# Linear attention on one core: V loads on the Activation queue, ten output buffers, stores three groups behind compute

## The chip, the cores and the metric

The kernel runs on one core of a Trainium2 chip. The metric is the device time of one execution in microseconds; a kernel is run several times and the median is quoted. A profile of one execution comes with each kernel; its span is about 1.8 us shorter than the time of that same execution. Executions over 1.5% slower than the fastest of the same kernel are left out of the means. A ratio is the mean time of one kernel's fast runs over that of the other's fast runs in the same rounds, so it is not quite the ratio of the medians.

The engines go by their names in the profile: PE multiplies matrices (PEld is its loading of weights), DVE is the vector engine, ACT the Activation (scalar) engine, POOL the general one, and SP issues transfers. A transfer (DMA) is issued by SP or ACT into that engine's queue, also called its ring or row, and moved in packets by 16 DMA engines. In a page's DMA row the span is cut into 40 slices, and each digit is the busy share of a slice in tenths (9 is 90% or more).

## The reference

Three float32 inputs of 8 x 12 heads x 512 rows x 64 columns, one output of the same shape.

```python
Q_feat = np.maximum(0, Q) + 1
K_feat = np.maximum(0, K) + 1
KV = np.einsum('bhkd,bhkv->bhdv', K_feat, V)
K_sum = np.sum(K_feat, axis=2)
numerator = np.einsum('bhqd,bhdv->bhqv', Q_feat, KV)
denominator = np.einsum('bhqd,bhd->bhq', Q_feat, K_sum)
return (numerator / (denominator[:, :, :, None] + 1e-10)).astype(np.float32)
```

There is little arithmetic per byte: 37.75 MB are read and 12.58 MB written.

## The kernel before

Four heads form a group; there are 24 groups. A group moves K, V and Q in and one output out, each as one transfer of 524,288 bytes (128 partitions x 2 runs of 2048 bytes). In iteration `it` the program prepares the features of group `it`, makes the products K'V and the transposes of Q for group `it-1`, divides and writes the output tile of group `it-2`, issues the loads of group `it+6` and the store of group `it-5`.

```python
IN_BUFS = 6
OUT_BUFS = 7
LAG = 5
...
    def load(g):
        k_raw = in_pool.tile([P, M, C, D], FP32, name="k_raw")
        ...
        nc.sync.dma_start(out=k_raw, in_=k_dram[:, sl])
        nc.sync.dma_start(out=v_raw, in_=v_dram[:, sl])
        nc.sync.dma_start(out=q_raw, in_=q_dram[:, sl])

    def store(g):
        nc.sync.dma_start(out=o_dram[:, g * M : g * M + M], in_=outs.pop(g))

    def features(g):
        ...   # kf on DVE (line 86), v_aug on ACT (line 89), qf on DVE (line 90)

    def kv_and_transpose(g):
        ...   # 32 small matmuls into kva_ps (line 107), copied by ACT (line 115);
        ...   # 8 transposes of qf into qt_ps (line 119), copied by ACT (line 121)

    def output(g):
        o_sb = out_pool.tile([P, M, C, D], FP32, name="o_sb")
        ...   # 32 small matmuls into o_ps (line 132); per half: reciprocal
        ...   # (line 142) and multiplication into o_sb (line 143), both on DVE

        for g in range(IN_BUFS):
            load(g)
        for it in range(NG + 2):
            if it < NG:
                features(it)
            if 1 <= it < NG + 1:
                kv_and_transpose(it - 1)
            if it >= 2:
                output(it - 2)
            if it + IN_BUFS < NG:
                load(it + IN_BUFS)
            s = it - 2 - (LAG - 2)
            if s >= 0:
                store(s)
        for s in range(NG + 2 - LAG, NG):
            store(s)
```

## Time and profile before

| what | value |
|---|---|
| time, median of 3 runs | 136.72 us (136.59 to 136.78) |
| busy: PE, DVE, ACT, SP's transfers | 44%, 51%, 40%, 99% of the span |
| transfers | 96 of 524,288 bytes, all on one queue |
| steady rate | 383 to 406 GB/s from 10 to 122 us |
| division waiting for a store to land | 38.5 us in 13 places |

Read it in this order: the DMA row shows that transfers bound the kernel, so idle time on an engine matters only where it delays a transfer. The prediction below shows the lines. One thing that it uses is in no summary line. A transfer runs on 16 DMA engines, and each reports its share with a count; the trace has the time of each count. The **last count** of a transfer is its landing. The **spread**, last count less first, is how far the slowest DMA engine is behind the fastest. I read a large spread at the end as the slowest engine still having work queued, so that it sets the end, and a spread of 0.2 us as all engines waiting for that transfer to be issued, so that compute sets the end.

### The profile page before, as it was taken

The numbers are of one execution on the slowest core, as the hardware profiler recorded it, in microseconds if no ns is written. First come the engines' busy times: TensorE is split into PE (matmuls) and PEld (weight loads), VectorE is DVE, ScalarE is ACT, GpSimd is POOL, SyncE is SP. The second block draws the span as 40 slices with busy tenths as digits, with TensorE's granted clock in tenths as the row PEclk, the third lists the DMA queues.
The fourth block names the chain that finished last, engine by engine and source line by source line (L and its number), as shares of the span: only waits on it lengthen the run. The fifth ranks groups of instructions, "written<-read, shape, count | busy, mean of one in ns | idle before, by whom it ended". The sixth has DMA issues, their size and how long they took to land.

```text
span 135.5 us, 3993 instructions
## 1 busy us (share of the span) xinstructions
PE 60.0 (44%) x1728; PEld 47.5 (35%) x1728; DVE 68.9 (51%) x144; ACT 53.9 (40%) x73; POOL 0.9 (1%) x9
## 2 busy tenths in 40 slices
PE   0033576635766510246156265264272543738520
PEld 0031454534555500135145054153251432526410
DVE  0223287656876500627538438348075272569760
ACT  3306434664446653051542533623605416143300
POOL 2000000000000000000000000000000000000000
DMA  4999999999999999999999999999999999999764
GB/s 128 353 348 398 387 387 387 384 387 387 383 386 385 387 383 399 403 400 399 387 402 400 396 404 400 396 402 397 406 400 396 404 402 397 403 402 367 298 251 155
DMA packets 26129, 50.58 MB, mean 373 GB/s; under 512 B 1537, under 2 KB 1537, under 8 KB 26113
## 3 DMA queue, kind: packets, MB, share of 16 engines
q1 hardware_dynamic: 26112, 50.34, 99.0%
q8 instruction: 13, 0.21, 0.6%
q14 instruction: 4, 0.02, 0.0%
HBM read 37.75 MB, written 12.58 MB: 372 GB/s over the span
## 4 chain that ended last, share of the span: by engine, by line
DMA 85%; DVE 8%; issue 1%; SPq 1%; PE 1%; DVEq 0%
DMA out_dram<-o_sb 55%; DMA q_raw<-in_Q_dram 16%; DMA v_raw<-in_V_dram 8%; DMA k_raw<-in_K_dram 6%; DVE o_sb L143 6%; DVE recip L142 1%; PE o_ps L132 1%; DVE kf L86 1%; DVE qf L90 1%; SPq L75 0%; SPq L76 0%; SPq L74 0%; DVEq L143 0%
## 5 line engine op out<-in xcount | busy, mean ns | idle before, releaser
L143 DVE TENSOR_TENSOR o_sb<-o_ps,recip 128x512 f32<-128x512 f32 x48 | 33.2, 692 | 39.7 <-DMA out_dram<-o_sb 38.5
L132 PE MATMUL o_ps<-kva,qt 64*64 64x65 bf16 x768 | 21.6, 244 | 48.7 <-DVE recip L142 37.8
L89 ACT CAST v_aug<-v_raw 128x1024 bf16<-128x1024 f32 x24 | 25.1, 1046 | 28.5 <-DMA v_raw<-in_V_dram 28.5
L132 PEld LDWEIGHTS <-qt 64*64 64x64 bf16 x768 | 15.6, 149 | 57.0 <-ACT v_aug L89 31.1
L121 ACT COPY qt<-qt_ps 128x1024 bf16<-128x1024 bf16 x24 | 24.3, 1014 | 9.8 <-PE qt_ps L119 9.8
L119 PE MATMUL qt_ps<-identity,qf 128*128 128x128 bf16 x192 | 24.8, 310 | 3.2 <-DVE qf L90 2.3
L90 DVE TENSOR_SCALAR qf<-q_raw 128x1024 bf16<-128x1024 f32 x24 | 16.5, 689 | 16.2 <-DMA q_raw<-in_Q_dram 16.2
L107 PE MATMUL kva_ps<-v_aug,kf 64*64 64x65 bf16 x768 | 15.7, 243 | 18.0 <-ACT kva L115 11.3
L119 PEld LDWEIGHTS <-qf 128*128 128x128 bf16 x192 | 18.5, 140 | 5.8 <-DVE qf L90 4.6
L107 PEld LDWEIGHTS <-kf 64*64 64x64 bf16 x768 | 13.4, 150 | 19.7 <-issue 17.8
L115 ACT CAST kva<-kva_ps 128x130 bf16<-128x130 f32 x24 | 6.4, 268 | 34.5 <-PE kva_ps L107 34.5
L86 DVE TENSOR_SCALAR kf<-k_raw 128x1024 bf16<-128x1024 f32 x24 | 16.4, 684 | 5.5 <-DMA k_raw<-in_K_dram 5.5
L142 DVE RECIPROCAL recip<-o_ps 128x8 f32<-128x8 f32 x48 | 9.6, 200 | 1.4 <-PE o_ps L132 1.4
L89 ACT ACT_TABLE_LOAD x1 | 1.3, 1283 | 0.7 <-PEq L185 0.7
masks.py:199 POOL TENSOR_SCALAR_AFFINE_SELECT identity<-identity 128x128 bf16<-128x128 bf16 x1 | 0.3, 292 | 0.1
L154 POOL MEMSET v_aug<- 128x32 bf16 x3 | 0.2, 127 | 0.0
masks.py:197 POOL MEMSET identity<- 128x128 bf16 x1 | 0.2, 206 | 0.3 <-POOLq L185 0.3
L185 POOL MEMSET const-bfloat16-1.0<- 128x1 bf16 x1 | 0.1, 101 | 0.0
L185 POOL MEMSET const-uint8-127<- 128x1 uint8 x1 | 0.1, 101 | 0.0
L185 POOL MEMSET const-float32-0.0<- 128x1 f32 x1 | 0.1, 98 | 0.2 <-issue 0.2
L185 POOL MEMSET const-float32-1.0<- 128x1 f32 x1 | 0.1, 98 | 0.0
## 6 DMA issues: line engine op xcount, KB each, us to landing
k_raw<-in_K_dram SPq DMA_DIRECT2D x24, 512.0 KB, 10.7
v_raw<-in_V_dram SPq DMA_DIRECT2D x24, 512.0 KB, 10.8
q_raw<-in_Q_dram SPq DMA_DIRECT2D x24, 512.0 KB, 10.8
out_dram<-o_sb SPq DMA_DIRECT2D x24, 512.0 KB, 10.4
```

The lines of the kernel that those rows point to most:

```text
L86: nc.vector.tensor_scalar(out=kf, in0=k_raw, scalar1=1.0, scalar2=1.0, op0=ALU.add, op1=ALU.max)
L89: nc.scalar.copy(out=v_aug[g % NV][:, :, :, 0:D], in_=v_raw)
L90: nc.vector.tensor_scalar(out=qf.rearrange("p c m d -> p m c d"), in0=q_raw, scalar1=1.0, scalar2=1.0, op0=ALU.add, op1=ALU.max,)
L107: nc.tensor.matmul(kva_ps[64 * m : 64 * m + 64, j, 0:D1], lhsT=kf[64 * j : 64 * j + 64, m, c, :], rhs=va[64 * j : 64 * j + 64, m, c, 0:D1] ...
L115: nc.scalar.copy(out=kva[:, :, 0:D1], in_=kva_ps[:, :, 0:D1])
L119: nc.tensor.transpose(qt_ps[:, c, :], qf[:, c, :, :], identity)
L121: nc.scalar.copy(out=qt, in_=qt_ps)
L132: nc.tensor.matmul(ops[m][64 * j : 64 * j + 64, c // 4, off : off + D1], lhsT=qt[64 * m : 64 * m + 64, c, 64 * j : 64 * j + 64], rhs=kva[6 ...
L142: nc.vector.reciprocal(out=recip, in_=cells[:, :, :, D:D1])
L143: nc.vector.tensor_tensor(out=o_sb[:, m].rearrange("p (b r) d -> p b r d", b=2), in0=cells[:, :, :, 0:D], in1=recip.to_broadcast([P, 2, 4, ...
L154: nc.gpsimd.memset(t[:, :, :, D:VP], 1.0)
L185: nc = _bacc.Bacc("TRN2", target_bir_lowering=False, num_devices=1)
```

## The change

The intent: take the waits for output buffers away, give stores to the queue sooner, and let a second queue share the issuing.

```diff
-OUT_BUFS = 7
-LAG = 5
+OUT_BUFS = 10
+LAG = 3
...
         nc.sync.dma_start(out=k_raw, in_=k_dram[:, sl])
-        nc.sync.dma_start(out=v_raw, in_=v_dram[:, sl])
+        nc.scalar.dma_start(out=v_raw, in_=v_dram[:, sl])
         nc.sync.dma_start(out=q_raw, in_=q_dram[:, sl])
```

(A blank line is added too, so line numbers after it are one higher in the changed kernel.)

## The prediction

> **What bounds the kernel now.** I read the page first: the 40 slices and the queue table.
>
> ```profile
> DMA  4999999999999999999999999999999999999764
> GB/s 128 353 348 398 387 387 387 384 387 387 383 386 385 387 383 399 403 400 399 387 402 400 396 404 400 396 402 397 406 400 396 404 402 397 403 402 367 298 251 155
> ...
> q1 hardware_dynamic: 26112, 50.34, 99.0%
> ```
>
> The DMA row is 9 from the second slice to the 37th. DVE, the busiest compute engine, works 51% of the span, ACT 40%, PE 44%. So the transfers are the bound: 96 of them (24 groups, each K, V, Q and one store), 524,288 bytes each, on one queue. Only the two ends are below 380 GB/s. The obvious hope lies in the last four slices (3.39 us each): against 400 GB/s they miss (33+102+149+245) x 3.39 = 1.8 MB, or 4.5 us.
>
> Next, the waits. The two longest of the whole kernel are these:
>
> ```profile
> DVE o_sb L143 <- DMA out_dram<-o_sb: 38.5, 13, 8.6
> PE o_ps L132 <- DVE recip L142: 37.8, 14, 8.5
> ```
>
> The division waits 38.5 us in 13 places for an output buffer whose store has not landed; PE waits behind it. With seven buffers and stores five iterations back, the buffer that output(it-2) wants is that of group it-9, whose store is issued at iteration it-4. This is the wait that the change is made to remove. But idle time of DVE costs only if it delays a transfer. So I read the waits of the DMA queue and its timeline. Each kind mostly waits there for its own kind (the store line for stores: 8.9 us in 12 places; K for K, V for V, Q for Q in 11 places each), and once stores flow, its own kind two groups back is eight transfers back: transfer n is issued when transfer n-8 has landed. Eight are in flight, so the median of 10.4 us from issue to landing is just 8 x 1.3 us of queueing. The rows of the timeline show the pace:
>
> ```profile
> 91.91 0.38 SPq L80 DMA_DIRECT2D out_dram<-o_sb  x1
> 93.24 1.44 SPq L74 DMA_DIRECT2D k_raw<-in_K_dram  x1
> 95.27 0.65 SPq L75 DMA_DIRECT2D v_raw<-in_V_dram  x1
> 96.58 0.56 SPq L76 DMA_DIRECT2D q_raw<-in_Q_dram  x1
> ...
> 108.97 0.62 SPq L80 DMA_DIRECT2D out_dram<-o_sb  x1
> ```
>
> An issue every 1.31 us, with one step of 2.03 us (93.24 to 95.27). The trace also records the 16 counts with which each transfer reports its landing. For each transfer I took the first and the last count. The first transfers have a spread of 0.27 us; the spread is 1.99 us at the third transfer, 2.4 us at 27 us, 3.4 us at 95 us and 4.3 us at 117 us. The last count comes at a steady 1.35 us per transfer while there are only loads, 1.31 us when mixed, 1.26 us among the last stores, and it jumps by an extra 0.55, 0.70 and 0.70 us near 27, 95 and 105 us, each time just after one of the 13 instruction packets (16,384 bytes, about 1.05 us each) in the trace. So the 16 DMA engines are not equal: one falls behind by 4.3 us, and **that slowest one sets every landing**.
>
> This changes the reading of the tail:
>
> ```profile
> core 0: us, PE busy (x) PEld busy (x) DVE busy (x) ACT busy (x) POOL busy (x), PEclk, DMA share, GB/s
> 119.50:122.00 2.50, 1.11 (x52) 0.92 (x56) 2.40 (x5) 0.62 (x1) 0.00 (x0) 1.00 1.05 399
> 122.00:125.00 3.00, 2.54 (x100) 2.04 (x92) 2.93 (x7) 1.28 (x2) 0.00 (x0) 1.00 0.95 363
> 128.00:132.00 4.00, 0.91 (x32) 0.67 (x32) 3.02 (x7) 0.00 (x0) 0.00 (x0) 1.00 0.74 282
> 132.00:134.00 2.00, 0.00 (x0) 0.00 (x0) 0.00 (x0) 0.00 (x0) 0.00 (x0) 1.00 0.63 239
> ```
>
> and of the DVE timeline, the last row (start, duration, what):
>
> ```profile
> 131.13 0.69 DVE L143 TENSOR_TENSOR o_sb<-o_ps,recip 128x512 f32<-128x512 f32 x1
> ```
>
> The DMA share falls after 122 us because the engines that are ahead run dry while compute (five output groups, freed only when a store landed at 119.47 us) catches up. The slowest engine does not run dry then: last counts come at 128.39, 129.63, 130.92 and 132.20 us, still 1.24 to 1.29 us apart. Only the last store is late: its tile is ready at 131.8 us, and it lands at 134.64 us, 2.44 us after the one before.
>
> **What the Trainium skill says.** "DMA: Bandwidth & Descriptors", section "Issuing engines are not separate DMA queues": transfers started by different engines run on the same 16 DMA engines and interleave; several issuers save only sequencer time. The trace of before agrees that this time isn't scarce: in the first 4.8 us an issue takes 0.43 to 0.47 us, against 1.3 us for the transfer. The same page, "Queues, rings and completion order": each DMA engine alternates between the rows it has work for, packet by packet. So V on its own row would overtake K and Q in the queue; one row in this trace can't show it. "Perfetto Trace Analysis", section "What 'DMA-bound' means": a DMA-bound kernel can be bound on specific DMA engines; the landing spread agrees. "Runtime: NRT & Kernel Launch", section "Instruction fetch mechanics", has instructions refilled in 16 KiB blocks by DMA and calls the cost mostly hidden; here 13 such packets appear, and the jumps say they are not hidden on the engine that carries them.
>
> **The change part by part.**
>
> V on the Activation queue. Moved: 24 issues of about 0.45 us, 11 us of ACT's time, in which it is 60% idle: nothing on the path. No byte less. If the n-8 rule spans both queues, as I expect, ACT now stands in these waits itself. At the start it must issue V of groups 0 to 5 before its first cast, and the V of group 5 waits for Q of group 2, the ninth transfer: about 9 to 11 landings, so the first cast comes at 14 to 17 us rather than 5.55 us. Compute has slack for this (about 3 us per group on DVE against 4.0 us for three loads), and no load before the one of group 9 needs anything that ACT made. Effect on the end: 0. The start has a stretch below 350 GB/s, in which the slowest engine lost 3.14 - 1.36 = 1.8 us at the third transfer. Two rows may shorten it, if it came from feeding one ring; I can't tell, and count 0.3 us.
>
> Ten output buffers. The buffer of output(it-2) is now that of group it-12. Removes the 38.5 us of DVE waiting nearly whole, none of it from the DMA path until the tail. There compute no longer stands five groups behind, so the last stores are ready in time. Worth on the slowest engine: 2.44 - 1.27 = 1.17 us.
>
> Stores three iterations back. The store of it-3 was computed before the features of iteration `it` on DVE, so it adds no wait. Ten stores instead of twelve follow the last loads: 10 x 1.26 = 12.6 us, in which compute has the last group's chain and at most three groups of about 2.9 us to do, some 9 us. It fits. Stores begin some 8 us sooner, when the pace improves from 1.35 to 1.31 us: six transfers x 0.04 = 0.2 us at most; I count 0.1.
>
> Sum: 1.17 + 0.3 + 0.1 = 1.6 us at best guess; a little given back to a second queue's waits and drain, say 0.2. 136.72 - 1.4 = 135.3 us.
>
> **The rivals.** First, **the whole tail is won**: all 4.5 us of missing bytes less about 1 us for the last landing, 3.5 us, 133.2 us. For it speaks the tail of the GB/s row; against it the counts of the slowest engine, which has no hole there. It could become true only if the two rows balance the engines too. Second, **ACT becomes a gate**: blocked on a V's landing it holds the transposed copies, so PE, DVE and at last the K loads; DMA engines starve near the start, and 1 to 3 us are lost: 137 to 139 us. For it speaks program order in ACT; against it that V, alone on its row, lands early, and that in the mixed phase it waits only for V two groups back, which is 10 us old. Third, **the mix of rows changes the pace of a packet**: 1 ns of some 82 ns is 1.6 us over 96 x 16 packets. The pace already differs between loads and stores, so either sign is possible. Fourth, nothing at all: the last landing is hidden by another late engine, 136.5 us.
>
> **Range and chances.** 135.3 us, with 133.6 to 136.9 us for 8 in 10: the lower end takes the head's 1.8 us or a packet 1 ns faster, the upper end the gate. 2% faster means under 134.0 us, which needs both the tail and most of the head or the pace: 0.15. Slower than 139.5 us needs a starved DMA: 0.04. Within 2%: 0.81.
>
> **What would show it.** In the changed profile: the wait of o_sb for out_dram under 5 us; the DMA row at 9 one or two slices longer; the last DVE work 6 us or more before the end of the span (before: 131.8 of 135.5 us); first cast on ACT at 14 to 17 us; ACT waiting for landings at its DMA issues; steady GB/s within 1% of 400; 13 or so instruction packets and a spread of about 4 us still there. I am wrong if the spread collapses (then nearer 133 us), if the DMA row shows holes before 45 us (slower), or if the mixed pace leaves 1.29 to 1.33 us per transfer.

## The result, and the profile after

The changed kernel takes 135.13 us (134.71 to 135.29, 4 runs) against 136.70 us before (136.59 to 136.78, 4 runs): ratio 0.9881, 95% interval 0.9857 to 0.9905. This is 1.6 us, within 2%, and close to the 135.3 us predicted.

The page of the changed kernel, DMA row, rate and queues:

```profile
DMA  4999999999999999999999999999999999999982
GB/s 111 398 392 387 387 387 384 388 386 384 387 384 387 387 403 392 398 399 398 400 395 401 398 400 395 400 402 397 406 408 392 407 401 400 407 397 407 401 344 88
...
q1 hardware_dynamic: 19584, 37.75, 75.0%
q10 hardware_dynamic: 6528, 12.58, 25.3%
q8 instruction: 13, 0.21, 0.6%
```

The row is at 9 for one slice more than before, the next is at 8, and its tail is short. A quarter of the packets (V) now runs on a queue of its own, q10, and there V overtakes K and Q, as the prediction expected. The last number is the median time from issue to landing; before it was 10.7, 10.8 and 10.8 us:

```profile
k_raw<-in_K_dram SPq DMA_DIRECT2D x24, 512.0 KB, 10.8
v_raw<-in_V_dram ACTq DMA_DIRECT2D x24, 512.0 KB, 8.2
q_raw<-in_Q_dram SPq DMA_DIRECT2D x24, 512.0 KB, 11.4
```

The instruction packets are still 13. The steady rate is what it was, near 387 GB/s with loads alone and near 400 GB/s mixed.

The longest waits of DVE and ACT for transfers in the changed kernel (who waited for what, us in total, times, longest):

```profile
DVE kf L87 <- DMA k_raw<-in_K_dram: 25.9, 18, 5.4
...
DVE qf L91 <- DMA q_raw<-in_Q_dram: 23.9, 23, 2.1
ACT v_aug L90 <- DMA q_raw<-in_Q_dram: 19.1, 7, 7.1
...
ACT v_aug L90 <- DMA out_dram<-o_sb: 8.0, 4, 3.7
ACT v_aug L90 <- DMA k_raw<-in_K_dram: 7.6, 4, 4.3
```

The division's wait for `out_dram`, 38.5 us before, is gone from the list. Apart from 2.9 us for PE, DVE now waits only for loads, which is what a kernel bound by transfers should look like. The cast of V, though, "waits" for Q, for K and for stores, none of which it reads: ACT stands in front of the V issue that precedes the cast in its program, until an older transfer has landed.

The last division starts at 126.03 us of 133.2, where it was 131.13 us of 135.5:

```profile
126.03 0.69 DVE L144 TENSOR_TENSOR o_sb<-o_ps,recip 128x512 f32<-128x512 f32 x1
```

Last counts and spreads show the two ends (computed from the trace's landing counts; times from the span's start, us):

| landing | before: last count, spread | after: last count, spread |
|---|---|---|
| 2nd | 5.53, 0.27 | 5.74, 0.37 |
| 3rd | 8.67, 1.99 | 8.20, 0.54 |
| 10th | 18.12, 1.64 | 16.84, 0.28 |
| 12th | 21.01, 1.88 | 19.55, 0.28 |
| 14th | 23.73, 1.87 | 23.69, 1.74 |
| 94th | 130.92, 1.47 | 129.87, 3.78 |
| 95th | 132.20, 0.25 | 131.13, 3.77 |
| 96th | 134.64, 0.19 | 132.38, 3.04 |

At the end, the last step was 2.44 us and is now 1.25 us, the pace of a store on the slowest engine; the spread of 3.04 us says that this engine had work to the last. At the start, the stall of 2 us at the third landing is gone, and at the tenth landing the changed kernel is 1.28 us ahead. But at the 14th the two are level again, within 0.04 us: between the 12th and the 14th landing the spread of the changed kernel jumps from 0.28 to 1.74 us. One instruction packet of 16,384 bytes ran at 20.49 us. So I read that this packet put one DMA engine 1.46 us behind. That was the first hint that the gain of the start may not reach the end.

### The profile page after: what moved, and what is told of

Read it like the earlier page. It is cut to its first block, busy times and chain, and to the rows that moved or that the text cites. A ratio compares the mean times of both kernels' runs of the same rounds, so it can differ in the third digit from the quotient of the medians.

```text
span 133.2 us, 3935 instructions
## 1 busy us (share of the span) xinstructions
PE 57.6 (43%) x1728; PEld 45.8 (34%) x1728; DVE 72.1 (54%) x144; ACT 53.5 (40%) x73; POOL 0.9 (1%) x9
## 2 busy tenths in 40 slices
DMA packets 26128, 50.58 MB, mean 380 GB/s; under 512 B 1536, under 2 KB 1536, under 8 KB 26112
## 4 chain that ended last, share of the span: by engine, by line
DMA 84%; DVE 8%; PE 1%; ACTq 1%; issue 1%; SPq 0%
DMA q_raw<-in_Q_dram 44%; DMA k_raw<-in_K_dram 26%; DMA v_raw<-in_V_dram 14%; DVE o_sb L144 4%; DVE qf L91 2%; PE o_ps L133 1%; DVE recip L143 1%; ACTq L76 1%; DVE kf L87 0%; SPq L75 0%; SPq L77 0%
## 5 line engine op out<-in xcount | busy, mean ns | idle before, releaser
L90 ACT CAST v_aug<-v_raw 128x1024 bf16<-128x1024 f32 x24 | 25.1, 1046 | 37.9 <-DMA q_raw<-in_Q_dram 19.1
L108 PEld LDWEIGHTS <-kf 64*64 64x64 bf16 x768 | 14.1, 150 | 52.8 <-issue 36.2
L133 PE MATMUL o_ps<-kva,qt 64*64 64x65 bf16 x768 | 19.5, 244 | 8.0 <-DVE o_sb L144 6.2
L120 PEld LDWEIGHTS <-qf 128*128 128x128 bf16 x192 | 18.5, 141 | 11.5 <-DVE qf L91 10.7
L133 PEld LDWEIGHTS <-qt 64*64 64x64 bf16 x768 | 14.2, 149 | 14.7 <-DVE o_sb L144 8.1
## 6 DMA issues: line engine op xcount, KB each, us to landing
k_raw<-in_K_dram SPq DMA_DIRECT2D x24, 512.0 KB, 10.8
```

The lines of the kernel that those rows point to most:

```text
L90: nc.scalar.copy(out=v_aug[g % NV][:, :, :, 0:D], in_=v_raw)
L108: nc.tensor.matmul(kva_ps[64 * m : 64 * m + 64, j, 0:D1], lhsT=kf[64 * j : 64 * j + 64, m, c, :], rhs=va[64 * j : 64 * j + 64, m, c, 0:D1] ...
L120: nc.tensor.transpose(qt_ps[:, c, :], qf[:, c, :, :], identity)
L133: nc.tensor.matmul(ops[m][64 * j : 64 * j + 64, c // 4, off : off + D1], lhsT=qt[64 * m : 64 * m + 64, c, 64 * j : 64 * j + 64], rhs=kva[6 ...
```

## The experiments

All kernels are correct unless it is said otherwise. The kernel before had medians of 136.53, 136.70 and 136.88 us in the three sets of rounds (e1 to e4, e5 to e8, e9 to e12). Times are medians; ratios are against the kernel before in the same rounds.

| kernel | queue of V | buffers, store distance | time, range (us) | ratio, 95% interval |
|---|---|---|---|---|
| before | SP | 7, 5 | 136.53, 136.09 to 137.78 (rounds of e1 to e4) | 1 |
| e1 | Activation | 7, 5 | 137.61, 137.38 to 137.72 | 1.0064, 1.0023 to 1.0105 |
| e2 | SP | 10, 3 | 135.30, 134.67 to 135.81 | 0.9893, 0.9849 to 0.9936 |
| e3 | SP | 10, 5 | 135.65, 135.23 to 136.67 | 0.9929, 0.9884 to 0.9974 |
| e4 | SP | 7, 3 | 135.31, 134.50 to 136.40 (and one slow run, 136.53) | 0.9890, 0.9836 to 0.9945 |
| e5 (the changed kernel again) | Activation | 10, 3 | 135.03, 134.84 to 135.31 | 0.9880, 0.9845 to 0.9914 |
| e6 (e2 again) | SP | 10, 3 | 135.27, 134.98 to 136.36 | 0.9907, 0.9867 to 0.9948 |
| e8, merged matmuls | Activation | 10, 3 | 133.28, 133.11 to 133.39 | 0.9747, 0.9717 to 0.9778 |
| e9, 4096-byte runs (wrong result) | Activation | 10, 3 | 130.04, 129.84 to 130.08 | 0.9492, 0.9464 to 0.9520 |
| e10, more PE instructions | Activation | 10, 3 | 142.37, 141.62 to 142.52 | 1.0388, 1.0355 to 1.0420 |
| e11, merged matmuls | SP | 10, 3 | 134.34, 133.49 to 135.15 | 0.9810, 0.9767 to 0.9854 |
| e12, late ACT | SP | 10, 3 | 134.86, 134.54 to 135.77 | 0.9858, 0.9824 to 0.9892 |

### Which part makes the gain: e1 to e4

**e1: V on the Activation queue alone.**

```diff
-        nc.sync.dma_start(out=v_raw, in_=v_dram[:, sl])
+        nc.scalar.dma_start(out=v_raw, in_=v_dram[:, sl])
```

> V loads on the Activation queue alone; seven output buffers and stores five iterations back as before. Theory A (two separate gains: the start gets 1.3 us from the second queue, the tail 1.2 us from buffers and store distance): the start is ahead of the kernel before as in the changed kernel (tenth landing near 16.8 us rather than 18.1 us), but the division still waits over 25 us for stores and the last landing still comes 2 us or more after the one before it; 135.4 to 136.0 us. Theory B (buffers and store distance do everything, the queue nothing): 136.7 us. Theory C (the queue does everything): 135.1 us.

It is slower than the kernel before, which none of the three theories had. Its page and waits have the old tail and the old wait:

```profile
DMA  4999999999999999999999999999999999999654
...
DVE o_sb L143 <- DMA out_dram<-o_sb: 33.6, 13, 7.9
```

The start is steady as in the changed kernel (tenth landing at 16.81 us), but the last three landings come at 130.77, 132.31 and 134.79 us with spreads of 1.14, 0.20 and 0.20 us: compute sets the end, and what was won at the start is waited away at the output buffers. In this tail every delay of compute counts, and one shows in the PE timeline (start, duration, what, in brackets the idle time before it and its releaser):

```profile
122.78 0.59 PE L132 MATMUL o_ps<-kva,qt 64*64 64x65 bf16 x25 [0.45 <-DVE o_sb L143]
124.94 0.27 PE L132 MATMUL o_ps<-kva,qt 64*64 64x65 bf16 x5 [1.56 <-issue]
```

In the middle of one group's 32 matmuls PE stops for 1.56 us and waits for nothing that the profile shows, while an instruction packet is moving (122.63 to 123.56 us). PE waiting for its own instructions is the likely reading. The kernel before has no such gap in its tail. That this gap is the whole 0.9 us (ratio 1.0064) is argued, not shown: the profiled execution of before took 137.24 us, 0.5 us more than the median of its kernel, so the two profiles can't be subtracted.

**e2: buffers and store distance, all on the SP queue.**

```diff
-OUT_BUFS = 7
-LAG = 5
+OUT_BUFS = 10
+LAG = 3
```

> Ten output buffers and stores three iterations back, all transfers on the SP queue. Theory A: the wait of the division for stores falls under 5 us, the last landing comes 1.25 to 1.35 us after the one before, the stall at the third transfer (spread near 2 us) is still there; 135.3 to 135.7 us. Theory B: 135.1 us, as the whole change. Theory C: 136.7 us.

It has the gain of the whole change within the noise, without the second queue. The page's DMA row, and the longest waits of ACT and DVE:

```profile
DMA  4999999999999999999999999999999999999982
...
ACT v_aug L89 <- DMA v_raw<-in_V_dram: 68.6, 24, 4.0
...
DVE qf L90 <- DMA q_raw<-in_Q_dram: 42.7, 24, 2.6
```

No wait for stores is left; ACT waits for V, and DVE for Q and K. The last landings come at 129.82, 131.10 and 132.38 us with spreads of 3.91, 3.92 and 2.79 us: the slowest DMA engine sets the end.

**e3: ten buffers alone**, and **e4: stores three iterations back alone.**

```diff
e3:
-OUT_BUFS = 7
+OUT_BUFS = 10
e4:
-LAG = 5
+LAG = 3
```

> Ten output buffers alone, stores five iterations back, SP queue. Theory A: the buffer wanted is one of a store issued seven iterations earlier rather than four, so the wait goes and the tail gains the same 1.2 us: 135.3 to 135.8 us. Rival: the store distance is what matters (twelve stores after the last load): 136.7 us.

> Stores three iterations back alone, seven output buffers, SP queue. Theory A: the buffer wanted is one of a store issued six iterations earlier rather than four, so most of the wait goes too: 135.3 to 135.9 us. Rival: seven buffers still hold compute back: 136.7 us.

Either half is enough, and both rivals fall. The reuse distance explains it. Before, a buffer came back four iterations after its store was issued; in e3 it is seven, in e4 six. In e3 no wait for stores is left, in e4 this one, none of its 15 over 0.6 us:

```profile
DVE o_sb L143 <- DMA out_dram<-o_sb: 8.3, 15, 0.6
```

The last step between landings is 1.27 us in both.

### What the second queue is worth: e5, e6, e12

**e5 and e6** are the changed kernel and e2 once more, side by side.

> The changed kernel once more, unaltered, beside the next kernel on the same chip. Theory A now (the buffers and the store distance make the gain, the second queue is worth nothing once they are there, except that it steadies the start): within 0.4 us of the next kernel, with a narrower range of times. Theory C (the second queue adds to it): faster than the next kernel by 0.8 us or more.

> Ten buffers and stores three iterations back with all transfers on the SP queue, unaltered, for the comparison with the run before it. Theory A: 135.0 to 135.6 us, spread of its times over 1 us, as the loss at the third transfer differs from one execution to the next. Theory C: 0.8 us or more slower than the changed kernel.

The medians differ by 0.24 us (ratios 0.9880 and 0.9907, with intervals that overlap widely). So once compute is out of the way of the end, this test resolves no gain from the second queue. The ranges do differ: 0.47 us with V on its own queue, 1.38 us without. The fast runs of the other kernels agree: 0.24 to 0.58 us for after, e1, e5, e8 and e9, and 1.1 to 1.9 us for e2, e3, e4, e6, e11, e12 and the kernel before in each set of rounds (though its first four runs lay within 0.19 us). (e7 and e10, which POOL and PE bound, have 0.8 and 0.9 us.) The profiles show what varies. With one queue the spread at the third landing is 0.79, 1.32, 1.45, 1.57, 1.99, 2.81 and 2.86 us in seven profiles (e2, e4, e12, e6, before, e3, e11); with two it is 0.36 to 0.61 us in seven (e5, e1, after, e8, e9, e10, e7).

And why does a start that is up to 2 us better end only 0 to 0.4 us sooner? The last landings are 132.38 us (after), 132.38 (e2), 132.50 (e6), 132.63 (e3) and 132.76 us (e4), with spreads of 3.5 to 3.9 us at the last landing but one in each: the stall delays several DMA engines by different amounts, the instruction packets delay others later, and at the end only the latest of 16 counts. That it is mostly another engine than the one stalled at the start fits these numbers, but the trace does not name the engine of a count, so it is an inference.

**e12: what steadies the start, two rings or the late start of ACT and PE?** With V on its queue ACT must first issue six loads, so its first cast starts at 10.43 us rather than 5.55 us. Here the queue is SP's alone, and ACT is held back by a tiny copy that reads Q of group 2.

```diff
+        late = const.tile([P, 8], FP32, name="late")
+        nc.scalar.copy(out=late, in_=raw[2][2][:, 0, 0, 0:8])
         for it in range(NG + 2):
```

> Ten buffers, stores three iterations back, all on the SP queue, and one tiny copy on ACT ahead of its first cast that waits for Q of group 2, so that ACT and PE start as late as with V on the Activation queue. What steadies the start? Theory Q (two rings are fed where one was): the spread at the third transfer is still 0.7 us or more, times range over 1 us. Theory L (the late start of ACT and PE, whose work or instruction fetches disturb the first transfers): the spread at the third transfer is 0.3 to 0.6 us, and the range of times is about 0.5 us.

The spread at the third landing is 1.45 us and the range 1.23 us, as with the other kernels on one queue. ACT's first cast starts at 16.45 us, later still than the 10.43 us aimed at, and the stall is there all the same. The late start of ACT and PE is not it; theory L falls. Theory Q is what is left of the two, but two rings also come with two issuing engines, and ACT's table load, which runs at 0.73 us in the kernels on one queue (e12 too) and at 9.13 us in the changed kernel, was not moved alone. So why a single queue stalls at its second or third transfer stays open.

### What sets the end now: e7 to e10

**e7: instructions on an idle engine.** 1536 one-element memsets on POOL.

```diff
+        scrap = const.tile([P, 8], FP32, name="scrap")
+        for _ in range(1536):
+            nc.gpsimd.memset(scrap[0:1, 0:1], 0.0)
```

> The changed kernel with 1536 one-element memsets added on POOL, which is idle and on which nothing waits; about six more instruction packets of 16,384 bytes. Theory F (the slowest DMA engine sets the end, and an instruction packet costs one engine some 1.5 us): the spread of the landings grows when an added packet falls on an engine already late, the last landing comes 0.8 to 3 us later, 136 to 138 us. Rival (only the sum of bytes counts, shared by 16 engines): 0.1 MB more is 0.25 us, 135.4 us.

This run missed. Its time, 253.02 us, is that of the memsets themselves (span 251.1 us, POOL at work to its end), and the packets came otherwise than I had thought:

```profile
q8 instruction: 13, 0.21, 0.3%
q14 instruction: 15, 0.12, 0.1%
```

POOL's instructions arrive as 12 more packets of 8192 bytes on q14 (there were 3 packets), each of 0.3 to 0.5 us, and only nine of the 15 ran within the time of the transfers. The last transfer landed at 132.14 us, no later than without them. It neither supports theory F nor, with packets a third as long, does it refute it.

**e8: fewer PE instructions.** The small matmuls are merged in pairs. One weight load takes the features of both m (128 columns); of the 128 x 130 result the two diagonal blocks are used. They go into a block-diagonal `kva_bd`, zeroed once, so that in the second product one matmul of 128 rows makes both m.

```diff
-            for m in range(M):
-                for j in range(2):
-                    nc.tensor.matmul(
-                        kva_ps[64 * m : 64 * m + 64, j, 0:D1],
-                        lhsT=kf[64 * j : 64 * j + 64, m, c, :],
-                        rhs=va[64 * j : 64 * j + 64, m, c, 0:D1],
+            for j in range(2):
+                nc.tensor.matmul(
+                    kva_ps[:, j, 0 : M * D1].rearrange("p (m x) -> p m x", m=M),
+                    lhsT=kf[64 * j : 64 * j + 64, c, :, :],
+                    rhs=va[64 * j : 64 * j + 64, :, c, 0:D1],
...
-        nc.scalar.copy(out=kva[:, :, 0:D1], in_=kva_ps[:, :, 0:D1])
+        kva = kva_bd[g % NV]
+        for m in range(M):
+            nc.scalar.copy(
+                out=kva[64 * m : 64 * m + 64, :, m, 0:D1],
+                in_=kva_ps[64 * m : 64 * m + 64, :, m * D1 : m * D1 + D1],
+            )
...
-                        ops[m][64 * j : 64 * j + 64, c // 4, off : off + D1],
-                        lhsT=qt[64 * m : 64 * m + 64, c, 64 * j : 64 * j + 64],
-                        rhs=kva[64 * m : 64 * m + 64, j, 0:D1],
+                        ops[64 * j : 64 * j + 64, r, 0 : M * D1].rearrange("p (m x) -> p m x", m=M),
+                        lhsT=qt[:, 4 * h + r, 64 * j : 64 * j + 64],
+                        rhs=kva[:, j, :, 0:D1],
```

(kf is laid out as (c, m, d); the division takes four c of both m at a time.)

> The changed kernel with both groups of small matmuls merged in pairs (one weight load of 128 columns for both m in the first, a block-diagonal right side with zeros in the second): 80 PE instructions per group rather than 144, so about 6 instruction packets rather than 13, the same data transfers and a correct result. Theory F: the slowest engine is delayed less, the spread falls under 3 us, the last landing comes 0.7 to 2.5 us sooner, 132.5 to 134.3 us. Rival (sum of bytes): 0.1 MB less is 0.25 us, 134.9 us. Rival (compute sets the tail): no change, as the last division is already over 5 us before the end.

```profile
span 131.5 us, 2451 instructions
...
DMA  4999999999999999999999999999999999999992
...
q8 instruction: 7, 0.11, 0.4%
```

At 133.28 us it beats both kernels: 1.75 us under the changed kernel of the same rounds. There are 7 instruction packets rather than 13; the 14th landing, level with before in the changed kernel, comes at 22.26 us with a spread of 0.35 us, as the first packet runs only at 25.62 us. At the end the spread is 2.3 us rather than 3.8 us, and the last landing comes at 130.71 rather than 132.38 us, 1.67 us sooner. Six packets fewer are 98,304 bytes, or 0.25 us at 400 GB/s, so the rival of the byte sum gives a seventh of it. The lag of the slowest DMA engine accounts for nearly all: the first count of the 95th landing comes at 127.16 us against 127.36 us in the changed kernel, so the fastest engine gains 0.2 us, but the last count comes at 129.47 against 131.13 us. Merging also changes the work of PE, ACT and DVE, so that the packets alone make the difference is the best reading, and not isolated by a run (e7 and e10 were to do it, and failed). Compute was not the end before (last division over 6 us earlier) and isn't now (123.7 us). PE is busier in this kernel, 71.5 us against 57.6 us, and its granted clock was 0.707 to 0.725 in all six executions. It was below 1 in all six of e11 (0.603 to 0.695) and of e12 (0.598 to 0.614), which has the PE work of the changed kernel, and 1.0 in every execution of the other kernels; no run shows why. It did not matter to the time, as PE is not the bound.

**e11: the merged matmuls with all transfers on the SP queue.**

> The kernel with merged matmuls, all loads and stores on the SP queue: the second queue's worth once more, now with few instruction packets. Theory A: within 0.6 us of the merged kernel with V on the Activation queue (133.3 us), but with a wider range of times and a spread near 1 to 2 us at the third transfer, so 133.3 to 134.2 us. Theory C: 134.2 us or more.

It is 134.34 us with a range of 1.66 us, and the profiled execution has a spread of 2.86 us at the third landing and 4.1 us near the end. Ratios to before are 0.9810 and 0.9747 (other rounds; the intervals, 0.9767 to 0.9854 and 0.9717 to 0.9778, just overlap). By the ranges set beforehand this is theory C's (134.2 us or more), by 0.14 us. So with fewer instruction packets to hide it, the stall of the single ring seems to reach the end, and the second queue is worth about 0.6%; rounds shared by both kernels would have to confirm it. It also limits what e8 says: against e12, with 13 packets on the same queue and in the same rounds, the merged kernel is only 0.5 us faster (ratios 0.9810 and 0.9858, intervals overlap), and its profiled execution, the slowest of its six, ends no sooner (last landing 132.55 against 132.35 us).

**e10: more PE instructions.** 32 one-column matmuls per group into an unused PSUM column.

```diff
+        for i in range(32):
+            nc.tensor.matmul(
+                kva_ps[0:64, 0, 128:129], lhsT=kf[0:64, 0, 0, :],
+                rhs=va[0:64, 0, 0, 0:1], start=True, stop=True,
+            )
```

> The changed kernel with 32 one-column matmuls added per group, into a PSUM column that nobody reads: 1536 more PE instructions, about six more instruction packets of 16,384 bytes (19 rather than 13), some 0.7 us more PE work per group, the same data and a correct result. Theory F (the slowest DMA engine sets the end and each instruction packet delays one engine by about 1.5 us): landing spread above 4 us at the end, last landing 0.8 to 2.5 us later, 135.8 to 137.5 us. Rival (sum of bytes): 0.1 MB more is 0.25 us, 135.3 us. Rival (PE latency): the last division ends later than 127.5 us.

The packets became 19 as expected, but the test is spoilt for theory F: 142.37 us, and PE is the bound. The added matmuls take 1.84 us per group rather than 0.7 us, and PE stops in its own stream:

```profile
DVE recip L151 <- PE o_ps L141: 45.5, 22, 4.0
...
PE kva_ps L108 <- issue: 10.6, 6, 2.2
...
PEld L116 <- issue: 9.1, 6, 2.2
```

PE and its weight loads wait up to 2.2 us at a time for nothing that the profile shows, and the last landings, at 137.17 and 139.65 us, have spreads of 0.2 us. The third expectation, that PE's latency reaches the end, is the one that came true. What it does show is that this kernel has little room for more PE instructions.

**e9: packets of 4096 bytes.** The same bytes, the same compute, other rows: 16 neighbouring rows per partition (the diff is shortened; the run adds this as a view of its own and indexes it by group). This mixes heads, so the result is wrong; it measures the transfers alone.

```diff
-        return t.flatten_outer_dims().rearrange("(n p c) d -> p n c d", p=P, c=C)
+        return t.flatten_outer_dims().rearrange("(n p m c) d -> p n m c d", p=P, m=M, c=C)
```

> The changed kernel with every transfer of the same bytes cut into runs of 4096 bytes instead of 2048 (each partition takes 16 neighbouring rows; the heads are then mixed, so the result is wrong on purpose; the compute is the same). Half as many packets. Theory P (part of each packet's 84 ns is a cost per packet): a 4096-byte packet takes under 160 ns, steady rate above 405 GB/s, 128 to 133 us. Rival (the engine's rate per byte is the limit): a packet takes 168 ns, 135 us.

```profile
span 128.2 us, 3935 instructions
...
DMA packets 13840, 50.58 MB, mean 395 GB/s; under 512 B 1536, under 2 KB 1536, under 8 KB 13824
```

A packet takes 159 ns (median) rather than 2 x 84 = 168 ns, so about 9 ns of each are a cost per packet (84 = a + b and 159 = a + 2b give a = 9), or of the shorter run in memory, which this run doesn't tell apart. The kernel is 5% faster than before, and about 4% faster than the changed kernel, which it edits (0.9492 / 0.9880 = 0.961; other rounds). Theory P holds. The Trainium skill, "Perfetto Trace Analysis", section "DMA Optimizations", advises batching small transfers, such as 2 KB into 4 or 8 KB. Here the transfers stay at 524,288 bytes and only their packets grow from 2048 to 4096 bytes; that gives the 4%. A correct kernel of this kind would need a head on 32 partitions instead of 64 and twice as many small matmuls; after e10 it is doubtful that it would keep the gain. It was not tried.

## Why the prediction was right

The time, 135.13 us, lies 0.2 us from the prediction, and its main step was right. By its own steps:

**The slowest DMA engine sets every landing.** Right, but for the last two of the kernel before. The changed kernel ends with a spread of 3 to 4 us and steps of 1.25 to 1.27 us to the last. e8 is the best evidence: with six packets fewer that delay single engines, the end moves by 1.67 us, six to seven times what their bytes would cost, and nearly all of it is lag of the slowest engine. The prediction took the jumps beside packets as 0.55 to 0.70 us, probably because it read them in the last counts alone, where an engine that is not the latest shows only part of its delay; the clean start of the changed kernel shows 1.46 us for its first packet.

**The tail is worth 1.17 us, not 3.5 or 4.5 us.** Right: the last step went from 2.44 to 1.25 us, which is 1.19 us. The prediction gave all of this to the ten buffers and 0.1 us to the store distance; e2, e3 and e4 show that either removes the wait and makes the gain. One reading was not exact: not only the last store was late. The last but one, issued at 129.37 us, landed 2.83 us later with a spread of 0.25 us, like the last one (2.79 us, 0.19 us), so compute set it too; that it came 1.28 us after its forerunner, the pace of the slowest engine, hid this. The two profiles differ by another 1.07 us at the landing before the last, which no step of the prediction explains; the profiled execution of before was 0.5 us over its median, so part of it may be that.

**V on the second queue is worth 0.3 us at the start.** Not shown in the time: e5 and e6 differ by 0.24 us, with intervals that overlap, so the 0.3 us (like the 0.1 us for earlier stores and the 0.2 us given back) is below what the runs resolve. That the sum came out so close is partly luck. The start did gain, 1.28 us at the tenth landing of these two profiles, and gave it back to an instruction packet by the 14th. The fourth rival, that a gain is hidden by another late engine, was written for the tail; it fits the start. e1 shows a cost that the prediction did not have: with the old buffers the second queue makes the kernel 0.6% slower; whether ACT as a gate or PE's late instructions cause it, no run decides.

**The first cast comes at 14 to 17 us.** That ACT issues six loads first and waits for landings there held; which landing was wrong: the cast came at 10.43 us. The prediction let eight transfers of both queues wait in one order. In the trace each queue had four in flight at the start (SP's fifth issue at 5.42 us, ACT's fifth at 5.76 us, both after the first two landings), so ACT's sixth issue waited for the fourth landing, at 8.71 us, and not for the ninth transfer. As the prediction had it, this made no difference to the end that the runs resolve. Stores began 5.0 us sooner (39.64 against 44.68 us), not 8 us.

**ACT as a gate; another pace of packets.** ACT did wait 47 us for landings at its issues (19.1 + 9.1 + 8.0 + 7.6 + 3.2), as the rival said; with the data loaded ahead it delayed no transfer that counted. The median packet takes 84 ns in both kernels.

## What to carry to other kernels

In a kernel bound by transfers, ask of each landing whether the slowest DMA engine or the issuer made it late: the spread of its counts tells, and the mean DMA share does not. A wait for buffers is worth what it adds to the last landing (here 38.5 us of waiting were 1.2 us of time), and either way of lengthening the reuse distance was enough. When nothing waits any more, look at what else the DMA engines carry: the kernels with fewer instructions (e8) and longer runs per packet (e9) gained more on top than the change had.

## What the Trainium skill lacked or had wrong

- "Runtime: NRT & Kernel Launch", section "Instruction fetch mechanics", calls the cost of a new instruction block mostly hidden. Here the slowest DMA engine fell 1.46 us further behind at one packet of 16,384 bytes, and a transfer-bound kernel with 7 packets instead of 13 was 1.75 us faster (e8; on one queue, e11 against e12, 0.5 us and not resolved). PE also stood still up to 2.2 us at a time in e10 with no releaser in the profile.
- The same section gives the refill block as 16 KiB. POOL's instructions came as packets of 8192 bytes on another queue (12 packets for 1536 instructions).
- "DMA: Bandwidth & Descriptors", section "Issuing engines are not separate DMA queues", says that several issuers save only issue time. For the median of the changed kernel this agrees (135.03 and 135.27 us). It does not have that one ring stalls at its first transfers by 0.8 to 2.9 us, differently in each execution, and two rings do not (0.36 to 0.61 us); the ranges of fast times are 0.2 to 0.6 us with two (0.8 and 0.9 us in e7 and e10) and 1.1 to 1.9 us with one, and with few instruction packets the second queue seems to gain 0.6%.
- No page gives the size to which the 16 DMA engines drift apart: near the end 4.3 us in the kernel before, 3.8 us in the changed one (4.5 us at most, at 98 us), 2.4 us in e8 and 4.1 us in e11, both with 7 instruction packets.
